# Reordering the second norm's transition: T4's products ahead of B22's, and the work of ScalarE, GpSimd and VectorE around them moved

## The chip, the cores and the metric

One core of one Trainium2 chip runs one launch of the kernel. The metric is the device time of the launch in microseconds. Before the change it is 1539.03 us, the median of three runs (1538.82 to 1541.5).

## What is computed

A bidirectional encoder block on one sequence of 1024 positions with 1024 channels, in float32. The change lies in its second half, the ConvFFN. Cut to that:

```python
h2 = rmsnorm(x, g_ffn) * (1 + scale2) + shift2
u = depthwise_conv_seq(h2 @ w_up, conv_w, conv_b)      # w_up: 1024 x 5632, 3 taps over positions
u_val, u_gate = jnp.split(u, 2, axis=-1)               # 2 x 2816 channels
x = x + gate2 * ((jax.nn.gelu(u_gate, approximate=True) * u_val) @ w_down)
return rmsnorm(x, g_final)
```

`scale2`, `shift2` and `gate2` come from the conditioning vector. `x` has by then the first half (two attentions, gates, `w_out`) added to it.

## The kernel before

**Precision.** A float32 product is made of three matmuls: each operand is split into a high part in fp32r (a copy on ScalarE) and a low part (operand minus high part, on VectorE or GpSimd), and TensorE (PE) adds high by high, high by low and low by high. `split` (lines 55 and 56) does this for weights.

**The up products.** `h2 @ w_up` runs as 22 jobs. A job makes 128 value channels and 128 gate channels of `u` for all 1024 positions, which are two halves of 512. So it is a 2 x 2 block product: weights a11, a12 (value) and a21, a22 (gate), the input halves over channels as blocks B11, B21 (first 512 positions) and two more blocks for the other positions. The kernel uses Strassen's scheme in Winograd's form, with seven block products in place of eight. The weight side needs S1 = a21 + a22, S2 = S1 - a11, S3 = a11 - a21 and S4 = a12 - S2, made on GpSimd (`FirstParts.sums`, `third`, `fourth`, lines 909, 910, 913 and 916, and `a_operands`, lines 884 to 886 and 891, for the later jobs). The input side needs T1, T2, T3, T4 and B22. The table `STEPS` pairs them: step 0 is a11 by B11, 1 is S2 by T2, 2 is S1 by T1, 3 is S3 by T3, 4 is a12 by B21, 5 is S4 by B22, 6 is a22 by T4. Each step is 12 matmuls of 128 x 512 in four chunks `k` (lines 950 to 952).

**PSUM.** `products` gives a job four banks, a to d, by the string `"abcdacd"`: step 5 adds onto the bank c that step 2 filled, and step 6 onto the bank d of step 3. Before step 5 may write, VectorE must have read step 2's value (line 963: `psum + v`, put into a spare bank); before step 6, it must have read step 3's (line 960, which makes `v`). After step 5 comes line 968, after step 6 line 971.

**The transition.** Jobs 0 and 1 start while the second half of the norm's input is still coming out of `w_out`. Their products run in lockstep, two generators `gens[0]` and `gens[1]`, in the order of steps 0, 4, 1, 3, 2, 5, 6, because T1 to T4 and B22 depend on the last sum of squares. `out_tile` finishes `m2[k]`, the second half of positions, unscaled; `scaled(k)` multiplies it by the norm's factor `bc`; `copied(k)` puts `m1[k]` (first half, scaled) into PSUM as `t2[k]`; `t2_sum` and `t2_low` make T2's high and low part, `t1_sum` and `t1_low` T1's, `t3_high` and `t3_low` T3's, `b22` (through `shifted`, lines 1078 and 1079) B22's, and `t4_sum` and `t4` (through `operand`, lines 864 and 865) T4's. The whole stretch is in `manual_schedule`: PE, ScalarE (ACT), VectorE (DVE) and GpSimd (POOL) each run their instructions in the order in which the code issues them, so the list of calls after `p0, p1 = first2` is the order on four engines at once. The queue of SyncE (SP), which issues the DMAs, is ordered by the scheduler. `advance(g)` and `next(g)` issue the next half or the rest of a step of a generator.

**The end of jobs 0 and 1.** `conv_in` (line 1163, ScalarE) and six taps (line 1169, VectorE) make the convolution of one half of the channels from four banks, line 1198 the Gelu of the gate half, line 1203 the gate times the value, line 1204 its store. `convs` holds four such pieces to be issued later; `held` keeps job 0's end until job 1's is done. Job 2 (`p2`) loads its two weight tiles into the slots that job 1's `raw[1]` tiles (`wraw`) leave. Jobs 3 to 21 and the product with `w_down` come after `late_others.close()`: there the scheduler orders ScalarE, VectorE and GpSimd by its own costs.

Of the kernel before, what the change touches and what calls it, by code (L numbers as in the profile page):

```python
# [10 lines left out]
FR = mybir.dt.float32r  # L11
AF = mybir.ActivationFunctionType
OP = mybir.AluOpType
# [3 lines left out]
S = 1024  # L17
# [11 lines left out]
def hybrid_encoder(tc, xT, c, w_ada, small, w_in, w_v, p1_bias, p23_bias, na_bias, ln2_mult, ident, w_br, w_out,  # L29
# [1117 lines left out]
    m2.append(half_tile())  # L1147
# [11 lines left out]
    with tc.tile_pool(name="up", bufs=2, reuse_waits="tile") as work:  # L1159
        held, convs = [], []  # L1160
# [16 lines left out]
        def up_products(t, st, seq=range(7)):  # L1177
            u, ys = [{}, {}], {i: big([128, S]) for i in range(2) if t == FF - 1}

            def done(i, hf, src):  # L1180
                u[i][hf] = src
                if len(u[i]) == 1 and t < 2:
                    return
                if t < 2:
                    convs.append(lambda: finish(i, hf))
                    return
                with tc.high_priority(offset=-300 if t == FF - 1 else 0):
                    finish(i, hf)

            def finish(i, hf):  # L1190
                if i not in ys:
                    ys[i] = big([128, S])
                for n in range(2) if t < 2 else (hf,):
                    conv_in(ys[i], up_order[t] + FF * i, n, u[i][n])
                if len(u[i]) == 2:
                    conv_taps(ys[i], up_order[t] + FF * i, u[i])
                if len(u[0]) + len(u[1]) == 4:
                    act.activation(ys[1], ys[1], AF.Gelu_apprx_tanh)  # L1198
                    if t == 0:
                        held.append((t, ys))  # L1200
                        return
                    for n, y in (*held, (t, ys)):
                        dve.tensor_tensor(y[0], y[0], y[1], OP.mult)  # L1203
                        sp.dma_start(a_scr[up_order[n]], y[0])
                    held.clear()
            spot, orders = None, {}
            if t < 2:
                spot, orders = (lambda: ps.tile([128, 512], FT, name="stage", tag=("pcol", "pbc")[t])), {2: (0, 2, 3, 1)}
            return products(st, 4, lambda n, k: late[n][k] if n in late else (ops[n][0][:, k], ops[n][1][:, k]), done,
                            seq, spot, orders)  # L1210

        gens = [up_products(t, sts[t], (0, 4, 1, 3, 2, 5, 6)) for t in range(2)]
# [26 lines left out]

        def t1_sum(k):  # L1240
            act.activation(m1[k], t2[k], AF.Copy)
            scaled(4 + k)
# [35 lines left out]
        copied(2)  # L1278
        scaled(0)
# [4 lines left out]
        p1.split_s(work)  # L1284
# [6 lines left out]
        pool.tensor_tensor(m2[3], m2[7], m2[3], OP.subtract)  # L1291
        p0.split_s3([work.tile([128, 2, 4, 128], FR, name=t, bufs=3) for t in ("wsh", "wsl")])
# [6 lines left out]
        p1.third()  # L1299
# [4 lines left out]
        t3_low(1)  # L1304
        t2_sum(3)
        t3_high(2)
        t2_low(3)
        t3_high(3)
        t3_low(2)
        advance(gens[0])  # L1310
        p1.split_s3(w_pair(4))
# [4 lines left out]
        p0.fourth()  # L1316
        p1.fourth()
        t1_sum(2)
        p0.split_s4()
        p1.split_s4()  # L1320
        t4_sum(0)
        t1_low(2)
        t1_sum(3)
        t4_sum(2)
        t1_low(3)
        t4_sum(3)
        t1_sum(1)
        t4_sum(1)
        advance(gens[0])
        t1_low(1)  # L1330
        advance(gens[1])
        next(gens[0])
# [11 lines left out]
        for k in range(4):  # L1344
            t4(k)
        next(gens[0])
        next(gens[1])
# [3 lines left out]
        convs.pop(0)()  # L1351
        p2.split_s(work)
        p2.split_s3([work.tile([128, 2, 4, 128], FR, name=t, bufs=3) for t in ("wsh", "wsl")])
        advance(gens[0])
        convs.pop(0)()
        p2.fourth()
        p2.split_s4()
        advance(gens[1])
        convs.pop(0)()
        convs.pop(0)()  # L1360
# [231 lines left out]
```

## Time and profile before

| | |
|---|---|
| median of three runs | 1539.03 us (1538.82 to 1541.5) |
| the profiled execution | 1538.77 us, its span 1537.0 us |
| PE busy | 1486.2 us, 97% of the span |
| VectorE, ScalarE, GpSimd busy | 992.0, 809.4 and 785.3 us (65%, 53%, 51%) |
| granted TensorE clock, mean | 0.986 |
| the transition | from 863 us of the span on; job 2's first product starts at 913.91 us |

The page gives busy time by engine over the whole span. PE is the engine that is nearly always busy, so time is lost where PE waits, and the views by window show where that is. A timeline row has the start, the duration, the line, the operation and its tiles, and in brackets how long the engine was idle before it and what ended that. Line numbers in rows are those of the kernel before.

### The profile page before, as it was taken

The page shows a single profiled execution, that of the slowest core. Times are in us where ns is not written, and L with a number is a line of the kernel's source. Part 1 is how long each engine was busy: PE and PEld are TensorE (multiplying, and loading weights), DVE is VectorE, ACT ScalarE, POOL GpSimd, SP SyncE. Part 2 cuts the span into 40 slices and gives each one's busy share as a digit, 9 for nine tenths or more (in the row PEclk, how much of TensorE's full clock was granted, in tenths as well). Part 3 has the DMA queues.
Part 4 walks back from the last instruction along what each step waited for, and adds up shares of the span by engine and source line. Part 5 has one row for each costly group of instructions (what it writes and reads, how often), then busy time and mean ns, then how long its engine had stood idle before and what let it go on. Part 6 is the DMA issues. An engine that isn't in the chain of part 4 may idle for free.

```text
span 1537.0 us, 21099 instructions
## 1 busy us (share of the span) xinstructions
PE 1486.2 (97%) x7512; PEld 1254.6 (82%) x7512; DVE 992.0 (65%) x1855; ACT 809.4 (53%) x1470; POOL 785.3 (51%) x506
## 2 busy tenths in 40 slices
PE   6999999999999999999999999999999999999998
PEld 5778888888888998888778777888888887878777
DVE  6673457676766655535534677777767778787765
ACT  5553656565765666644345545444444447476542
POOL 3524434333224444311156788877666675878721
PEclk7899999999999999999999999999999999999999
DMA  9857234423445565555544212322222224614323
GB/s 341 329 217 266 71 102 130 113 74 107 120 112 140 146 163 138 179 167 199 190 130 142 85 54 98 110 83 82 96 90 83 82 76 171 216 52 143 98 55 110
DMA packets 110305, 205.98 MB, mean 134 GB/s; under 512 B 40276, under 2 KB 55508, under 8 KB 110164
## 3 DMA queue, kind: packets, MB, share of 16 engines
q1 hardware_dynamic: 109928, 204.38, 41.0%
q8 instruction: 59, 0.97, 0.3%
q14 instruction: 46, 0.38, 0.1%
q10 hardware_dynamic: 272, 0.26, 0.0%
HBM read 159.51 MB, written 42.47 MB: 131 GB/s over the span
## 4 chain that ended last, share of the span: by engine, by line
PE 76%; DVE 7%; POOL 5%; DMA 4%; ACT 4%; issue 3%; SPq 1%; DVEq 0%; POOLq 0%; ACTq 0%
PE pj L79 11%; PE pj L78 11%; PE pj L77 11%; PE pj L952 9%; PE pj L951 9%; PE pj L950 9%; PE pj L467 2%; PE O L768 2%; POOL wlo L56 2%; DMA wraw<-w_down 2%; PE T L756 1%; PE b L247 1%; PE b L248 1%; PE S L735 1%; PE b L249 1%
## 5 line engine op out<-in xcount | busy, mean ns | idle before, releaser
L56 POOL TENSOR_TENSOR wlo<-wraw,whi 128x1024 fp32r<-128x1024 f32 (+1 forms) x80 | 188.2, 2353 | 225.3 <-ACT whi L55 224.1
L78 PE MATMUL pj<-h,whi 128*128 128x512 f32 x448 | 178.0, 397 | 0.0
L79 PE MATMUL pj<-h,wlo 128*128 128x512 f32 x448 | 178.0, 397 | 0.0
L77 PE MATMUL pj<-h,whi 128*128 128x512 f32 x448 | 177.9, 397 | 0.0
L1169 DVE SCALAR_TENSOR_TENSOR big<-pj,sm,big 128x512 f32<-128x512 f32 (+2 forms) x258 | 132.1, 566 | 31.3 <-ACT big L1163 31.1
L56 POOL TENSOR_TENSOR wsl<-big,wsh 128x1024 fp32r<-128x1024 f32 (+1 forms) x44 | 107.5, 2443 | 49.8 <-ACT wsh L55 49.8
L1163 ACT ACTIVATE big<-pj,sm 128x512 f32<-128x512 f32 x86 | 64.7, 776 | 118.9 <-DVE pj L968 51.8
L55 ACT ACTIVATE whi<-wraw 128x1024 fp32r<-128x1024 f32 (+1 forms) x80 | 81.8, 1022 | 85.0 <-PE pj L78 35.6
L79 PEld LDWEIGHTS pj<-h,wlo 128*128 128x128 f32 x448 | 84.4, 188 | 14.4
L78 PEld LDWEIGHTS pj<-h,whi 128*128 128x128 f32 x448 | 84.4, 188 | 14.1
L77 PEld LDWEIGHTS pj<-h,whi 128*128 128x128 f32 x448 | 84.3, 188 | 13.7
L538 POOL TENSOR_TENSOR vv<-vv 96x256 fp32r<-96x256 f32 (+2 forms) x32 | 41.2, 1297 | 98.8 <-ACT vv L537 97.6
L594 ACT ACTIVATE P<-P,st 128x256 f32<-128x256 f32 x128 | 64.3, 503 | 51.1 <-DVE st L593 50.8
L593 DVE CUSTOM_DVE_ANT_0 P<-S,bias 128x256 f32<-128x256 f32 x128 | 52.4, 421 | 42.7 <-PE S L640 23.8
L746 POOL TENSOR_SCALAR P<-P,stb 128x288 f32<-128x288 f32 (+1 forms) x32 | 39.9, 1247 | 66.4 <-DVE stb L743 59.2
L55 ACT ACTIVATE wsh<-big 128x1024 fp32r<-128x1024 f32 (+1 forms) x44 | 44.2, 1005 | 44.6 <-POOL big L885 26.2
L474 POOL TENSOR_SCALAR qb<-qs 128x256 fp32r<-128x256 f32 x32 | 26.4, 850 | 71.6 <-PE S L640 58.7
L1203 DVE TENSOR_TENSOR big<-big 128x1024 f32<-128x1024 f32 x22 | 45.7, 2076 | 22.0 <-ACT big L1198 22.0
L891 DVE TENSOR_TENSOR wraw<-wraw,big 128x384 f32<-128x384 f32 (+1 forms) x20 | 33.0, 1650 | 41.2 <-POOL big L885 39.6
L599 DVE TENSOR_TENSOR tl<-T,th 128x512 fp32r<-128x512 f32 x64 | 43.7, 688 | 23.4 <-ACT th L598 22.9
L950 PE MATMUL pj<-T2hi,wsh 128*128 128x512 f32 x124 | 48.8, 394 | 4.5 <-ACT T2hi L1234 3.2
L56 POOL TENSOR_TENSOR wsl<-wraw,wsh 128x768 fp32r<-128x768 f32 (+1 forms) x22 | 50.5, 2298 | 4.4 <-ACT wsh L55 4.4
(389 smaller groups left out, 4794.1 us busy)
## 6 DMA issues: line engine op xcount, KB each, us to landing
t<-w_ada SPq DMA_DIRECT2D x40, 512.0 KB, 6.7
wraw<-w_in SPq DMA_DIRECT2D x32, 512.0 KB, 5.6
big<-w_up SPq DMA_DIRECT2D x22, 512.0 KB, 5.0
wraw<-w_up SPq DMA_DIRECT2D x22, 512.0 KB, 3.6
as<-big SPq DMA_DIRECT2D x22, 512.0 KB, 2.6
big<-as SPq DMA_DIRECT2D x22, 512.0 KB, 6.9
wraw<-w_down SPq DMA_DIRECT2D x24, 384.0 KB, 4.1
gs<-gs SPq DMA_DIRECT2D x32, 256.0 KB, 2.0
```

The lines of the kernel that those rows point to most:

```text
L55: act.activation(hi, raw, AF.Copy)
L56: lo_eng.tensor_tensor(lo, raw, f(hi), OP.subtract)
L77: pe.matmul(psum, whi[:, k0 + k], mhi, start=k == 0, stop=False)
L78: pe.matmul(psum, whi[:, k0 + k], mlo, start=False, stop=False)
L79: pe.matmul(psum, wlo[:, k0 + k], mhi, start=False, stop=k == n - 1)
L593: dve.tensor_tensor_reduce(pp, d, bias, -1.0, BIG, OP.add, OP.min, mi)
L594: act.activation(pp, pp, AF.Exp, bias=mi, scale=-1.0, accum_out=li)
L950: pe.matmul(psum, whi[:, k], bhi, start=j < 4 and i == 0, stop=False, skip_group_check=True)
L951: pe.matmul(psum, whi[:, k], blo, start=False, stop=False, skip_group_check=True)
L952: pe.matmul(psum, wlo[:, k], bhi, start=False, stop=i == n - 1, skip_group_check=True)
L1163: act.activation(y[:, halves[hf]], src, AF.Identity, bias=conv[:, 3, t:t + 1], scale=conv[:, 1, t:t + 1])
L1169: dve.scalar_tensor_tensor(y[:, dst], src, wt, y[:, dst], OP.mult, OP.add)
```

## The change

The seven steps of jobs 0 and 1 now run in the order 0, 4, 1, 3, 2, 6, 5, so T4's products come before B22's. T4's parts are issued before B22's on ScalarE and GpSimd, and `fourth` and `split_s4` (S4 of both jobs) after T4's. `third` and `split_s` of job 1 and `split_s3` of both jobs are issued earlier, the copies that keep `m1[k]` (`t2_kept`, part of `t1_sum` before) in one group, the scaling of `m2[4..7]` earlier than the T1 sums that read it. `m2[7]` lies in a tile of `wide` in place of `half_tile`. The convolutions' parts are now four dictionaries: `cins` (copies), `taps`, `gelus`, `ends2` (gate and store), issued in a new interleaving with job 2's weights, the gate half of each job first. No instruction is added or left out: each engine issues as many as before.

```diff
--- before.py
+++ after.py
@@ -1144,7 +1144,7 @@
     late_others.enter_context(tc.manual_schedule(engines={act.engine, dve.engine, pool.engine}))
     first2[1].sums()
     first2[1].split11(pool)
-    m2.append(half_tile())
+    m2.append(wide())
     sq = out_tile(1, KT - 1, sqa, m2[KT - 1])
     mpool.release()
     oppool2 = tc.alloc_tile_pool(name="ops2", bufs=1, side="right", reuse_waits="tile")
@@ -1157,7 +1157,11 @@
     late = {n: [] for n in ("B22", "T4")}
 
     with tc.tile_pool(name="up", bufs=2, reuse_waits="tile") as work:
-        held, convs = [], []
+        cins, taps, gelus, ends2 = {}, {}, {}, {}
+
+        def gated(t, ys):
+            dve.tensor_tensor(ys[0], ys[0], ys[1], OP.mult)
+            sp.dma_start(a_scr[up_order[t]], ys[0])
 
         def conv_in(y, t, hf, src):
             act.activation(y[:, halves[hf]], src, AF.Identity, bias=conv[:, 3, t:t + 1], scale=conv[:, 1, t:t + 1])
@@ -1182,7 +1186,11 @@
                 if len(u[i]) == 1 and t < 2:
                     return
                 if t < 2:
-                    convs.append(lambda: finish(i, hf))
+                    ys[i] = big([128, S])
+                    cins[t, i] = lambda: [conv_in(ys[i], up_order[t] + FF * i, n, u[i][n]) for n in range(2)]
+                    taps[t, i] = lambda: conv_taps(ys[i], up_order[t] + FF * i, u[i])
+                    gelus[t] = lambda: act.activation(ys[1], ys[1], AF.Gelu_apprx_tanh)
+                    ends2[t] = lambda: gated(t, ys)
                     return
                 with tc.high_priority(offset=-300 if t == FF - 1 else 0):
                     finish(i, hf)
@@ -1190,26 +1198,19 @@
             def finish(i, hf):
                 if i not in ys:
                     ys[i] = big([128, S])
-                for n in range(2) if t < 2 else (hf,):
-                    conv_in(ys[i], up_order[t] + FF * i, n, u[i][n])
+                conv_in(ys[i], up_order[t] + FF * i, hf, u[i][hf])
                 if len(u[i]) == 2:
                     conv_taps(ys[i], up_order[t] + FF * i, u[i])
                 if len(u[0]) + len(u[1]) == 4:
                     act.activation(ys[1], ys[1], AF.Gelu_apprx_tanh)
-                    if t == 0:
-                        held.append((t, ys))
-                        return
-                    for n, y in (*held, (t, ys)):
-                        dve.tensor_tensor(y[0], y[0], y[1], OP.mult)
-                        sp.dma_start(a_scr[up_order[n]], y[0])
-                    held.clear()
+                    gated(t, ys)
             spot, orders = None, {}
             if t < 2:
                 spot, orders = (lambda: ps.tile([128, 512], FT, name="stage", tag=("pcol", "pbc")[t])), {2: (0, 2, 3, 1)}
             return products(st, 4, lambda n, k: late[n][k] if n in late else (ops[n][0][:, k], ops[n][1][:, k]), done,
                             seq, spot, orders)
 
-        gens = [up_products(t, sts[t], (0, 4, 1, 3, 2, 5, 6)) for t in range(2)]
+        gens = [up_products(t, sts[t], (0, 4, 1, 3, 2, 6, 5)) for t in range(2)]
 
         def advance(g):
             for j in g:
@@ -1237,9 +1238,10 @@
             dve.scalar_tensor_tensor(ops["T2"][1][:, k], t2[k], shift2[:, 4 + k:5 + k], f(ops["T2"][0][:, k]), OP.add,
                                      OP.subtract)
 
+        def t2_kept(k):
+            act.activation(m1[k], t2[k], AF.Copy)
+
         def t1_sum(k):
-            act.activation(m1[k], t2[k], AF.Copy)
-            scaled(4 + k)
             dve.tensor_tensor(t2[k], m2[4 + k], t2[k], OP.subtract)
             act.activation(ops["T1"][0][:, k], t2[k], AF.Copy)
 
@@ -1276,59 +1278,68 @@
         advance(gens[0])
         bc = bcast(r, ps, "pbc")
         copied(2)
+        p1.third()
+        p1.split_s(work)
         scaled(0)
         t2_sum(0)
         scaled(1)
         t2_sum(1)
         advance(gens[1])
-        p1.split_s(work)
+        pool.tensor_tensor(m2[3], m2[7], m2[3], OP.subtract)
+        p0.split_s3([work.tile([128, 2, 4, 128], FR, name=t, bufs=3) for t in ("wsh", "wsl")])
         t2_low(0)
         scaled(2)
         t2_sum(2)
         t2_low(1)
         advance(gens[0])
         advance(gens[1])
-        pool.tensor_tensor(m2[3], m2[7], m2[3], OP.subtract)
-        p0.split_s3([work.tile([128, 2, 4, 128], FR, name=t, bufs=3) for t in ("wsh", "wsl")])
+        t2_kept(0)
+        scaled(4)
         t1_sum(0)
         t2_low(2)
         t1_low(0)
         copied(3)
         next(gens[0])
         next(gens[1])
-        p1.third()
         scaled(3)
         t3_high(0)
         t3_high(1)
         t3_low(0)
         t3_low(1)
+        p1.split_s3(w_pair(4))
         t2_sum(3)
         t3_high(2)
+        t3_high(3)
+        scaled(6)
         t2_low(3)
-        t3_high(3)
+        for k in (2, 3, 1):
+            t2_kept(k)
+        for k in (0, 2, 3, 1):
+            t4_sum(k)
         t3_low(2)
         advance(gens[0])
-        p1.split_s3(w_pair(4))
         t3_low(3)
         advance(gens[1])
         next(gens[0])
         next(gens[1])
-        p0.fourth()
-        p1.fourth()
         t1_sum(2)
-        p0.split_s4()
-        p1.split_s4()
-        t4_sum(0)
+        scaled(7)
         t1_low(2)
         t1_sum(3)
-        t4_sum(2)
+        scaled(5)
         t1_low(3)
-        t4_sum(3)
         t1_sum(1)
-        t4_sum(1)
+        t4(0)
+        t4(1)
         advance(gens[0])
         t1_low(1)
         advance(gens[1])
+        t4(2)
+        t4(3)
+        p0.fourth()
+        p1.fourth()
+        p0.split_s4()
+        p1.split_s4()
         next(gens[0])
         next(gens[1])
         b22(0)
@@ -1341,23 +1352,27 @@
         p2 = FirstParts(raw.pop(2), sts[2])
         p2.sums()
         p2.third()
-        for k in range(4):
-            t4(k)
-        next(gens[0])
-        next(gens[1])
         p2.split11(pool)
         advance(gens[0])
         advance(gens[1])
-        convs.pop(0)()
+        cins[0, 1]()
+        taps[0, 1]()
+        cins[1, 1]()
         p2.split_s(work)
+        advance(gens[0])
+        taps[1, 1]()
         p2.split_s3([work.tile([128, 2, 4, 128], FR, name=t, bufs=3) for t in ("wsh", "wsl")])
-        advance(gens[0])
-        convs.pop(0)()
+        advance(gens[1])
+        cins[0, 0]()
+        gelus[0]()
+        taps[0, 0]()
+        cins[1, 0]()
+        gelus[1]()
+        taps[1, 0]()
         p2.fourth()
         p2.split_s4()
-        advance(gens[1])
-        convs.pop(0)()
-        convs.pop(0)()
+        ends2[0]()
+        ends2[1]()
         late_others.close()
         for t in range(FF):
             nxt = iter(())
```

Three places in the built order. GpSimd, from job 1's S3 on (`wsl`, `wlo` and the split `big` tiles are low parts of weights, line 1261 or 1263 the four T4 sums, line 865 T4's low parts, line 909 job 2's first sum). Before:

```order
L913 TENSOR_TENSOR wraw_8352<-wraw_8350,wraw_8352 128x512
L56 TENSOR_TENSOR wlo_8567<-wraw_8352,whi_8566 128x1024
L916 TENSOR_TENSOR big_8229<-big_8229,big_8354 128x512
L916 TENSOR_TENSOR wraw_8350<-wraw_8350,big_8366 128x512
L56 TENSOR_TENSOR big_8598<-big_8229,big_8598 128x512
L56 TENSOR_TENSOR big_8601<-wraw_8350,big_8601 128x512
L1261 TENSOR_TENSOR big_7742<-big_7742,big_7740 128x512
L1261 TENSOR_TENSOR big_7743<-big_7743,big_7741 128x512 x2
L1261 TENSOR_TENSOR big_7742<-big_7742,big_7740 128x512
L909 TENSOR_TENSOR big_8685<-wraw_8683 128x512
L910 TENSOR_TENSOR big_8685<-big_8685,wraw_8681 128x512
L913 TENSOR_TENSOR wraw_8683<-wraw_8681,wraw_8683 128x512
```

Now:

```order
L913 TENSOR_TENSOR wraw_8352<-wraw_8350,wraw_8352 128x512
L56 TENSOR_TENSOR wsl_8468<-big_8366,wsh_8467 128x1024
L1288 TENSOR_TENSOR x2_8191<-wc_8373,x2_8191 128x512
L56 TENSOR_TENSOR wsl_8494<-big_8231,wsh_8493 128x1024
L56 TENSOR_TENSOR wlo_8554<-wraw_8352,whi_8553 128x1024
L1263 TENSOR_TENSOR big_7742<-big_7742,big_7740 128x512
L1263 TENSOR_TENSOR big_7743<-big_7743,big_7741 128x512 x2
L1263 TENSOR_TENSOR big_7742<-big_7742,big_7740 128x512
L865 TENSOR_TENSOR x2_8611<-big_7742,x2_8610 128x512
L865 TENSOR_TENSOR x2_8615<-big_7742,x2_8614 128x512
L865 TENSOR_TENSOR x2_8636<-big_7743,x2_8635 128x512
L865 TENSOR_TENSOR x2_8640<-big_7743,x2_8639 128x512
```

L913 has moved ahead of the low part of job 1's S2, the T4 sums ahead of the two L916 (S4), and T4's four low parts, which followed job 2's weight sums, ahead of S4 as well; S4's two differences and their low parts, and then job 2's weights, come after these rows.

ScalarE, at the high parts of T1, T4 (line 864) and B22 (line 1078); the `big` rows of line 55 are S4's high parts. Before:

```order
L55 ACTIVATE big_8598<-big_8229 128x512
L55 ACTIVATE big_8601<-wraw_8350 128x512
L1241 ACTIVATE big_7741<-pj_8531 128x512
L1244 ACTIVATE T1hi_8410<-pj_8531 128x512
L1241 ACTIVATE big_7740<-stage_8449 128x512
L1244 ACTIVATE T1hi_8410<-stage_8449 128x512
L1078 ACTIVATE x2_8649<-x2_8233,ada_66 128x512
L1078 ACTIVATE x2_8653<-x2_8272,ada_66 128x512
L1078 ACTIVATE x2_8665<-x2_8311,ada_66 128x512
L1078 ACTIVATE x2_8677<-x2_8373,ada_66 128x512
L864 ACTIVATE x2_8689<-big_7742 128x512
L864 ACTIVATE x2_8693<-big_7742 128x512
```

Now:

```order
L1246 ACTIVATE T1hi_8410<-stage_8449 128x512
L864 ACTIVATE x2_8610<-big_7742 128x512
L864 ACTIVATE x2_8614<-big_7742 128x512
L864 ACTIVATE x2_8635<-big_7743 128x512
L864 ACTIVATE x2_8639<-big_7743 128x512
L55 ACTIVATE big_8645<-big_8229 128x512
L55 ACTIVATE big_8648<-wraw_8350 128x512
L1078 ACTIVATE x2_8665<-x2_8233,ada_66 128x512
L1078 ACTIVATE x2_8669<-x2_8272,ada_66 128x512
L1078 ACTIVATE x2_8681<-x2_8311,ada_66 128x512
L1078 ACTIVATE x2_8693<-wc_8373,ada_66 128x512
L55 ACTIVATE whi_8705<-wraw_8697 128x1024
```

S4's high parts and B22's four rows stood ahead of T4's and now follow them; the copies of line 1241 that stood between T1's rows are gone from here.

SyncE's queue, the weight loads of jobs 2 (the first two rows), 3 (`big`) and 4 (`wraw_8820`, `wraw_8822`). Before:

```order
L1108 DMA wraw_8681<-w_up 128x1024
L1108 DMA wraw_8683<-w_up 128x1024
L1108 DMA wraw_8820<-w_up 128x1024
L1108 DMA wraw_8822<-w_up 128x1024
L1108 DMA big_8816<-w_up 128x1024
L1108 DMA big_8818<-w_up 128x1024
```

Now:

```order
L1108 DMA wraw_8697<-w_up 128x1024
L1108 DMA wraw_8699<-w_up 128x1024
L1108 DMA wraw_8820<-w_up 128x1024
L1108 DMA big_8816<-w_up 128x1024
L1108 DMA big_8818<-w_up 128x1024
L1108 DMA wraw_8822<-w_up 128x1024
```

Job 3's two loads have moved ahead of job 4's second.

## The prediction

> **What bounds the kernel now.** I read the page first, then PE's windows and waits, then one engine at a time. The page names the engine that matters, by busy time and by the chain that ended last:
>
> ```profile
> PE 1486.2 (97%) x7512; PEld 1254.6 (82%) x7512; DVE 992.0 (65%) x1855; ACT 809.4 (53%) x1470; POOL 785.3 (51%) x506
> PE 76%; DVE 7%; POOL 5%; DMA 4%; ACT 4%; issue 3%; SPq 1%; DVEq 0%; POOLq 0%; ACTq 0%
> ```
>
> So only time in which PE stands still, or runs at a lower clock, can go. By window (the transition in two parts, then steady jobs):
>
> ```profile
> core 0: us, PE busy (x) PEld busy (x) DVE busy (x) ACT busy (x) POOL busy (x), PEclk, DMA share, GB/s
> 863.20:902.00 38.80, 32.90 (x144) 26.17 (x143) 29.08 (x39) 23.91 (x39) 30.08 (x19) 0.96 0.10 34
> 902.00:946.00 44.00, 41.96 (x175) 33.52 (x175) 31.97 (x53) 23.38 (x29) 33.22 (x18) 0.96 0.28 96
> 960.00:1060.00 100.00, 100.00 (x443) 82.81 (x442) 71.57 (x105) 44.88 (x54) 73.15 (x40) 1.00 0.27 90
> ```
>
> Steady jobs leave PE no gap: 443 matmuls in 100 us, 0.226 us each. The transition leaves 38.80 - 32.90 = 5.9 and 44.00 - 41.96 = 2.0 us. PE's waits there, 863 to 946 (total, times, longest), and their places in its timeline:
>
> ```profile
> PE pj L950 <- ACT T2hi L1234: 3.2, 1, 3.2
> PE pj L950 <- DVE stage L963: 2.4, 1, 2.4
> PE pj L950 <- ACT wc L956: 1.1, 1, 1.1
> PE pj L952 <- POOL wsl L56: 0.7, 1, 0.7
> 883.14 0.50 PE L950 MATMUL pj<-T2hi,wsh 128*128 128x512 f32 x1 [3.15 <-ACT T2hi L1234]
> 885.18 0.63 PE L950 MATMUL pj<-T2hi,wsh 128*128 128x512 f32 x1
> 888.60 0.39 PE L952 MATMUL pj<-T3hi,wsl 128*128 128x512 f32 x1
> 901.28 0.47 PE L950 MATMUL pj<-x,big 128*128 128x512 f32 x1 [2.35 <-DVE stage L963]
> 902.29 0.63 PE L951 MATMUL pj<-x,big 128*128 128x512 f32 x1
> 905.68 0.40 PE L950 MATMUL pj<-x,big 128*128 128x512 f32 x1
> 914.36 0.39 PE L952 MATMUL pj<-B11hi,wlo 128*128 128x512 f32 x1
> ```
>
> Two waits matter: T2's last chunk, and S4 by B22 waiting for VectorE's line 963. Behind each a stretch of 3.4 us runs at half rate (0.63 us a matmul, 885.18 to 888.60 and 902.29 to 905.68), which costs 1.7 us each. 914.36 is job 2's third matmul, the first that needs its `wlo`; I measure the change there, because everything before it is jobs 0 and 1.
>
> **The first wait.** The chain behind it, on VectorE, GpSimd and ScalarE:
>
> ```profile
> 875.45 0.70 DVE L1243 TENSOR_TENSOR pj<-x,pj 128x512 f32<-128x512 f32 x1 [0.98 <-ACT big L1241]
> 878.01 3.74 DVE L1253 SCALAR_TENSOR_TENSOR T3lo<-x,cols,T3hi 128x512 fp32r<-128x512 f32 x2
> 881.68 0.69 DVE L1233 TENSOR_TENSOR pj<-pj,x 128x512 f32<-128x512 f32 x1
> 883.79 0.74 DVE L1253 SCALAR_TENSOR_TENSOR T3lo<-x,cols,T3hi 128x512 fp32r<-128x512 f32 x1
> 877.12 2.42 POOL L56 TENSOR_TENSOR wsl<-big,wsh 128x1024 fp32r<-128x1024 f32 x1
> 879.48 1.73 POOL L913 TENSOR_TENSOR wraw<-wraw 128x512 f32<-128x512 f32 x1
> 873.86 1.07 ACT L55 ACTIVATE wsh<-big 128x1024 fp32r<-128x1024 f32 x1
> ```
>
> Two T3 low parts, 0.74 us alone, took 3.74: they span the two GpSimd operations (to 879.54, and 879.48 to 881.21) and end after them; the T2 sum follows at 881.68. The new order puts L913 and `p1.split_s` earlier, and ScalarE's copy of 873.86 ahead of the T2 and T1 copies. VectorE's 0.98 of waiting at 875.45 falls away, so the T3 low parts start at 877.06; GpSimd is then idle, until ScalarE has written the high part of job 1's S3, some 878.4. The two take 2 x 0.66, the T2 sum starts at 878.4, T2's high part is there at 879.8 by the same distance as before (881.68 to 883.14), its low part 0.7 later. PE is ready for the high part at 883.14 - 3.15 = 880.0 and one matmul later, at 880.2, for the low part: a wait of 0.3 in place of 3.15, none if VectorE is a little earlier, all of it back if GpSimd again overlaps. I take 0.3, since the overlap is gone from the order.
>
> **PE up to S4.** From 880.5 it has 8 matmuls of T2, then 24 each of T3, T1 and T4: 80 x 0.226 = 18.1. It wants B22's step at 898.6.
>
> **GpSimd up to S4.** This engine has the longest list. Its rows of before, and the ScalarE and VectorE rows that stand between:
>
> ```profile
> 888.23 1.28 POOL L916 TENSOR_TENSOR big<-big 128x512 f32<-128x512 f32 x1
> 893.25 5.04 POOL L1261 TENSOR_TENSOR big<-big 128x512 f32<-128x512 f32 x4
> 903.31 5.47 POOL L865 TENSOR_TENSOR x<-big,x 128x512 fp32r<-128x512 f32 x4
> 908.74 2.42 POOL L56 TENSOR_TENSOR wlo<-wraw,whi 128x1024 fp32r<-128x1024 f32 x1
> 898.39 1.66 ACT L864 ACTIVATE x<-big 128x512 fp32r<-128x512 f32 x3
> 897.28 3.24 DVE L1079 SCALAR_TENSOR_TENSOR x<-x,ada,x 128x512 fp32r<-128x512 f32 x2
> 900.45 0.69 DVE L963 TENSOR_TENSOR stage<-pj,wc 128x512 f32<-128x512 f32 x1
> 909.28 3.09 DVE L1169 SCALAR_TENSOR_TENSOR big<-pj,sm,big 128x512 f32<-128x512 f32 x6
> ```
>
> Job 1's S3 low part runs 878.4 to 880.8, the four T4 sums (5.04, with 0.45 twice for overlap, as L913 took 1.73 where L916 takes 1.28) to 886.7. T4's first high part cannot start before ScalarE has copied T1's k=1, whose sum is VectorE's eleventh operation after 880.5 (0.6 to 0.7 apart, about 7.5): 888.0, plus 0.6 and 0.55 (1.66 / 3): 889.1. Now GpSimd runs without a pause: four line-865 low parts 5.0 to 894.1, two L916 2.5 to 896.6. Then S4's high part and B22's first high parts on ScalarE (0.63 + 0.64) to 897.9, two B22 low parts on VectorE, L963 behind them. GpSimd makes S4's low parts at that moment, so the pair costs between 1.4 (alone) and 3.24 (as at 897.28); I take 2.4. L963 ends at 897.9 + 2.4 + 0.7 = 901.0 and PE waits 901.0 - 898.6 = 2.4, just as long as before: L963 still stands behind two B22 low parts. B22's 24 matmuls take 5.4, or 7.1 with a slow stretch: job 2's third matmul could start at 906.9 to 908.6.
>
> **Job 2's weights.** More rows, for the next parts: the gate product, a wait of the taps for ScalarE, the S4 low part of job 2, job 3's load and what it held up, and the loads of `w_up` (KB, median us to landing):
>
> ```profile
> L1203 DVE TENSOR_TENSOR big<-big 128x1024 f32<-128x1024 f32 x22 | 45.7, 2076 | 22.0 <-ACT big L1198 22.0
> 928.20 0.75 DVE L1169 SCALAR_TENSOR_TENSOR big<-pj,sm,big 128x512 f32<-128x512 f32 x1 [2.52 <-ACT big L1163]
> 918.02 1.29 POOL L56 TENSOR_TENSOR big<-wraw,big 128x512 fp32r<-128x512 f32 x1 [0.90 <-ACT big L55]
> 919.76 6.06 DMA big<-w_up
> 929.20 2.41 POOL L56 TENSOR_TENSOR wlo<-big,whi 128x1024 fp32r<-128x1024 f32 x1 [9.88 <-ACT whi L55]
> wraw<-w_up SPq DMA_DIRECT2D x22, 512.0 KB, 3.6
> ```
>
> S4's low parts end at 896.6 + 2.5 = 899.1 and free the second load slot; a load takes 3.6 (last row), 902.8; L909, L910 and L913 3.8, 906.6; `wlo` 2.42, 909.0. GpSimd ends later than PE, so job 2's third matmul starts at 909.0 in place of 914.36: 5.4 earlier. The bounds: at PE's 906.9 it is 7.5. With 0.45 of overlap in each of four operations it is 3.6, and with 6.06 for the load in place of 3.6 also, 1.1. I take 5.4, because the load moves 512 KB with the queue otherwise empty there (10% DMA share in the first window).
>
> The rule in the Trainium skill's "SBUF — State Buffer" (section "Who interferes with whom") is that VectorE and GpSimd share one port pair under an exclusive lock. The rows at 878.01 and 879.48 agree (3.74 for 1.4, 1.73 for 1.28). By it B22's third and fourth low parts could hold GpSimd up once more, 2 x 0.74, and job 2's gain would be 3.9, between the forecast and the second rival.
>
> **VectorE in job 2.** Now all 24 taps are run straight after B22, and two gate products (L1203) stand between job 2's line 958 and 963. From 901.0: two B22 low parts and a L963 1.9, two L971 1.2, 0.9 for ScalarE's copies, 24 taps 12.0 (3.0 between six at 909.28), two L968, a L958 and a L960 2.4, two products 2.4, L963 0.7: 922.5. PE's step 5 of job 2, 58 matmuls after the third, stands at 909.0 + 13.1 = 922.1. That costs 0.4, or nothing, or 2.2 if the products run at their mean. So two chains, GpSimd's and VectorE's, allow about the same gain.
>
> The L1203 row's 2076 is the mean ns; I counted 1.2, two inputs of 1024 columns against 0.69 for 512, as no GpSimd work that overlaps is sure to be due then.
>
> **Job 3 and later.** SP issued job 3's loads at 919.76, behind a load of job 4 that waited for job 2's S4 low part (918.02); GpSimd then stood idle for 9.88. Now they go ahead of it, as soon as job 2's `wlo` and two `wsl` are done, 909.0 + 2 x 2.4 = 913.8: 5.9 earlier, with PE 5.0 earlier. The two waits at the next hand-over (1.1 + 0.7) stay: 0, bounds -1.5 to +2. `m2[7]`'s other tile and the order that the scheduler gives jobs 3 to 21 cost nothing while PE is covered as in 960:1060; after them 0, bounds -2 to +2.
>
> **Sum.** -5.4 + 0.4 = -5.0. The profiled execution took 1538.77, so 1533.8; the median (1539.03) stands 0.26 above it: 1534.0.
>
> **Rivals.**
> 1. *Faster still.* The lists of GpSimd and VectorE both run some 2 us shorter, and PE's floor of 906.9 (gain 7.5) or, with no wait at S4, 904.5 (9.9) holds: 1531.5 or 1529.1. For it: GpSimd's overlaps were guessed. Against: both have to give.
>    Does the 2.4 us wait slow PE's clock here? In the rows above, gaps of 3.15 and 2.35 were both followed by a slow stretch; with one, this rival's gain is 5.8. "TensorE: Matmul & The Clock Gate" in the Trainium skill (section "HAM oscillation") has as its rule that only gaps over some 3.4 us matter; by it the gain would be 7.5 in full. The trace disagrees.
> 2. *Same.* T2's wait comes back, or the load takes 6.06: gain 1 to 3, 1536 to 1538. For it: GpSimd has no slack in the list above, each lock adds 0.45.
> 3. *Slower.* VectorE is the bound. If each of the four groups of taps waits for ScalarE as at 928.20 (2.52), and the products run at 2.08, VectorE's L963 of job 2 comes 10.1 + 1.7 later, 934.3; PE waits 12.2 there, of which 5.4 were gained: 1539.0 + 6.8 = 1545.8. It decides from 927.5 on, where before's PE stood at this step. Against it: all copies are issued ahead of their taps, and ScalarE was 23.38 busy of 44.
>
> **Chances.** Forecast 0.70 (1532 to 1536), rival 1 0.10, rival 2 0.15, rival 3 0.05. The range runs from half of rival 1 to most of rival 2, 1530.0 to 1537.5. What the measurement tells from no change is about 0.2%, 3.1 us: forecast and rival 1 are faster by that (0.80), rival 2 is the same (0.15), rival 3 slower (0.05).
>
> **What would show it.** Right: PE's wait at T2's k=3 under 1 us and no slow stretch at 885; a wait of 1.5 to 3 us on L963 at the start of the last B22 step; the four line-865 rows on GpSimd without a gap before S4's; job 2's third matmul 4.5 to 6 us earlier than 914.36; SP's `big` loads near 914. Wrong: a T3 low part of over 1.5 us, a w_up load of over 5 us near 899, or a wait on L963 or L960 in job 2's steps 5 and 6.

## The result

The first comparison has six runs of each kernel: 1530.26 us median (1527.08 to 1531.87) after, 1539.25 (1538.82 to 1541.5) before, ratio 0.9936, interval 0.9922 to 0.9951. That is 9.0 to 9.9 us faster, where 5.0 was forecast; by the ratio the time is 1529.2 to 1529.4, some 0.7 below the lower end of the range. The same kernel was run twice more (e5_again, e11_third below): 0.9968 and 0.9974. All 28 runs of it have a mean of 1532.4 (standard deviation 2.9), 78 runs of the kernel before 1538.2 (2.2): 5.8 us apart, with 1.2 either way (twice the root of 2.9²/28 + 2.2²/78). By comparison the means lie 9.8, 5.2 and 4.2 us apart. The last two were made on two different chips, and that of the first is not on record; what a chip adds was not tested.

The profiled execution of the changed kernel took 1531.87, span 1530.1, that is 6.9 us less. Busy time on its page, by engine:

```profile
PE 1484.6 (97%) x7512; PEld 1254.6 (82%) x7512; DVE 964.2 (63%) x1855; ACT 807.9 (53%) x1470; POOL 777.9 (51%) x506
```

The two windows of the transition, columns as in the prediction (span, PE busy, and so on to the clock):

```profile
863.20:902.00 38.80, 36.08 (x159) 28.94 (x158) 26.79 (x41) 23.72 (x39) 30.30 (x20) 0.98 0.10 34
902.00:946.00 44.00, 42.65 (x179) 33.37 (x178) 36.13 (x54) 25.06 (x31) 40.28 (x23) 0.98 0.31 109
```

PE's waits from 863 to 946 us (total, times, longest):

```profile
PE pj L950 <- ACT x L1078: 2.4, 1, 2.4
PE pj L950 <- DVE wc L960: 0.7, 1, 0.7
PE pj L951 <- DVE T2lo L1238: 0.3, 1, 0.3
PE pj L950 <- DVE big L1173: 0.3, 1, 0.3
PE pj L952 <- POOL wsl L56: 0.2, 1, 0.2
```

PE's idle time fell from 5.9 and 2.0 to 2.7 and 1.35 us, and T2's 3.15 is gone. The 2.4 is the wait at S4 by B22: the copy of line 1078 that it names is the fourth (to 899.98), while the product begins with the first chunk; line 963, done at 899.83, frees its bank. The 0.7 for line 960 comes at 943.08, in job 3. The rows of its timeline behind that, several engines in order of time (line numbers of the changed kernel, each some lines off the old ones):

```profile
875.44 1.41 DVE L1255 SCALAR_TENSOR_TENSOR T3lo<-x,cols,T3hi 128x512 fp32r<-128x512 f32 x2
876.97 2.39 POOL L56 TENSOR_TENSOR wlo<-wraw,whi 128x1024 fp32r<-128x1024 f32 x1 [2.05 <-ACT whi L55]
879.33 5.96 POOL L1263 TENSOR_TENSOR big<-big 128x512 f32<-128x512 f32 x4
887.98 5.04 POOL L865 TENSOR_TENSOR x<-big,x 128x512 fp32r<-128x512 f32 x4 [2.70 <-ACT x L864]
896.83 2.40 DVE L1079 SCALAR_TENSOR_TENSOR x<-x,ada,x 128x512 fp32r<-128x512 f32 x2 [8.12 <-ACT x L1078]
899.15 0.68 DVE L963 TENSOR_TENSOR stage<-pj,wc 128x512 f32<-128x512 f32 x1
899.99 0.59 PE L950 MATMUL pj<-x,big 128*128 128x512 f32 x1 [2.44 <-ACT x L1078]
901.54 1.34 POOL L909 TENSOR_TENSOR big<-wraw 128x512 f32<-128x512 f32 x1 [3.52 <-DMA wraw<-w_up]
905.47 2.41 POOL L56 TENSOR_TENSOR wlo<-wraw,whi 128x1024 fp32r<-128x1024 f32 x1
907.93 0.50 PE L952 MATMUL pj<-B11hi,wlo 128*128 128x512 f32 x1
```

The two T3 low parts take 1.41 in place of 3.74, since GpSimd is idle until 876.97. Read the GpSimd rows downwards: S3's low part, T4's sums, T4's low parts, then S4's differences (to 895.52) and low parts (to 898.02), a wait of 3.52 for job 2's load, job 2's sums and its `wlo` to 907.88, and PE's first use of that at 907.93, in job 2's third matmul.

To compare executions I cut each at four places. *Entry* is the start of the transposes that spread the norm's factor for the first half of the positions (827.75 us before); the change touches little ahead of it. *Lead* is how far ahead PE then is in the steady jobs: matmuls counted from there on, against the same stretch of before, times 0.2267 us. *Later* is what is added up to the last norm's first narrow matmul (1500.75 before), *end* the rest. All in us against the profile of before, negative is faster; a count can be off by one matmul.

| kernel | entry | lead | later | end |
|---|---|---|---|---|
| changed, first profile | -1.7 | -5.0 | -3.2 | +3.0 |
| changed, e5_again | +0.5 | -5.0 | -2.9 | 0.0 |
| changed, e11_third | -2.9 | -5.0 | -1.2 | +1.4 |
| e1 early moves only | -0.2 | -3.8 | -0.4 | 0.0 |
| e6 new ending only | +2.1 | -2.5 | -1.2 | +0.2 |
| e9 step order only | -3.4 | +3.8 | -3.1 | 0.0 |
| e7 early moves and ending | -1.8 | -4.3 | +1.0 | -0.1 |
| e3 early moves and order | +1.7 | +0.3 | -1.5 | +0.1 |
| e2 order and ending | +1.1 | -0.8 | -0.3 | -0.1 |
| e8 T4's low parts on VectorE | -3.6 | -9.2 | -2.4 | -0.2 |
| e10 the same, two more moves | -0.2 | -9.7 | -2.9 | -0.1 |

The lead is the same 5.0 in three profiles. What differs between runs lies outside it. (e4 has no row: its narrow matmuls at the end are fewer; its lead is 4.7.)

### The profile page after: what moved, and what is told of

Same layout as the page of the kernel before. It is cut to its first block, busy times and chain, and to the rows that moved or that the text cites. A ratio compares the mean times of both kernels' runs of the same rounds, so it can differ in the third digit from the quotient of the medians.

```text
span 1530.1 us, 21118 instructions
## 1 busy us (share of the span) xinstructions
PE 1484.6 (97%) x7512; PEld 1254.6 (82%) x7512; DVE 964.2 (63%) x1855; ACT 807.9 (53%) x1470; POOL 777.9 (51%) x506
## 4 chain that ended last, share of the span: by engine, by line
PE 74%; POOL 8%; DVE 6%; issue 4%; DMA 4%; ACT 3%; SPq 0%; DVEq 0%; POOLq 0%; ACTq 0%
PE pj L79 11%; PE pj L77 11%; PE pj L78 11%; PE pj L952 8%; PE pj L950 8%; PE pj L951 8%; POOL wsl L56 2%; PE pj L467 2%; PE O L768 2%; POOL wlo L56 2%; DMA wraw<-w_down 2%; PE T L756 1%; PE S L735 1%; PE b L247 1%; PE b L249 1%
## 5 line engine op out<-in xcount | busy, mean ns | idle before, releaser
L968 DVE TENSOR_TENSOR pj<-pj,wc 128x512 f32<-128x512 f32 x34 | 23.6, 694 | 52.0 <-PE pj L952 51.9
L79 PE MATMUL pj<-mhi,wlo 128*128 128x512 f32 x128 | 50.2, 392 | 2.0 <-POOL wlo L56 2.0
L78 PE MATMUL pj<-mlo,whi 128*128 128x512 f32 x128 | 50.0, 391 | 0.0
```

The costliest lines, as they stand in the source:

```text
L78: pe.matmul(psum, whi[:, k0 + k], mlo, start=False, stop=False)
L79: pe.matmul(psum, wlo[:, k0 + k], mhi, start=False, stop=k == n - 1)
```

## The experiments

**The three parts of the change, one at a time.** `first_only` is the kernel before with the early moves:

```diff
         copied(2)
+        p1.third()
+        p1.split_s(work)
...
         advance(gens[1])
-        p1.split_s(work)
+        pool.tensor_tensor(m2[3], m2[7], m2[3], OP.subtract)
+        p0.split_s3([...])
         t2_low(0)
```

(with `third` and the last two lines taken from their old places, and `m2[7]` in a tile of `wide`).

> The kernel before with the early moves alone: L913 and the split of job 1's S2, and the split of job 0's S3, earlier, and the last tile in its new place; B22 still ahead of T4, the old ending. Lead is counted from PE's place at 863 us to its place in the steady jobs, 960 to 1290 us; the changed kernel has 5.0 there. Theory of the prediction (two lists, GpSimd's to job 2's first low part and VectorE's with the taps, bound the start and the middle of job 2, and T2's wait only starts them earlier): the wait at T2's k=3 falls from 3.15 to under 0.5, the wait on L963 stays 2 to 2.6, the lead is 3 to 3.5, since everything after T2 starts that much earlier in the old order too. Rival 1 (the step order 6, 5 makes the gain): the lead is under 1.5, the T2 time comes back as a longer wait on L963. Rival 2 (T2's wait with its slow stretch is the whole gain): 4.5 to 5.

Measured: ratio 0.9986 (0.9974 to 0.9999), 1535.4 median of 12 runs. Lead 3.8. Its largest waits from 863 to 955 us:

```profile
PE pj L950 <- ACT x L864: 2.6, 1, 2.6
PE pj L950 <- DVE wc L958: 1.6, 1, 1.6
```

T2's wait is gone, 1.6 of it is back as a wait for VectorE's line 958, and the wait at S4 by B22 is as before (the row names line 864; line 963 is what must be read there). No stretch runs at half clock, where the kernel before had two of 1.7 us each: 3.4 of the lead's 3.8 is that. The lead lies above the theory's 3 to 3.5 and below the second rival's 4.5 to 5: T2's wait with its slow stretch is not the whole gain, and more than the theory had comes with it.

`second_only` is the changed kernel with these moves undone (the same lines, the other way; `m2[7]` stays in its tile of `wide`).

> The changed kernel with the early moves undone: L913, job 1's S2 split, the T4 difference of m2 and job 0's S3 split back at their old places; the steps 0, 4, 1, 3, 2, 6, 5, T4 ahead of S4, and the new ending stay. Theory: T2's wait is back at 3.15 with its slow stretch at 885, GpSimd's list starts some 3.5 us later, and the lead from 863 to 960 us is 1.5 to 2; a wait of 1 to 3 us at job 2's start on its weights. Rival 1 (the step order makes the gain): 3.5 or more. Rival 2 (T2 is the whole gain): 0 within 0.5.

Measured: ratio 0.9985 (0.9972 to 0.9997). Lead 0.8, between the theory and the second rival. T2's wait returns with its half-clock stretch, and GpSimd's list is late: S4's second difference ends at 902.22, 3.9 us later than in the changed kernel with the entries (2.8 apart) taken off. That is met once more at job 2's start, in the second row (what ended that wait is taken up behind the experiments):

```profile
PE pj L950 <- ACT T2hi L1235: 3.1, 1, 3.1
PE pj L950 <- ACT wsh L55: 1.5, 1, 1.5
```

`old_end` is the changed kernel with copies, taps and Gelus interleaved as before:

```diff
         taps[0, 1]()
-        cins[1, 1]()
         p2.split_s(work)
-        advance(gens[0])
-        taps[1, 1]()
         p2.split_s3([...])
-        advance(gens[1])
+        advance(gens[0])
+        cins[1, 1]()
+        taps[1, 1]()
+        p2.fourth()
+        p2.split_s4()
+        advance(gens[1])
         cins[0, 0]()
...
```

> The changed kernel with the copies, taps and Gelus of jobs 0 and 1 in the old interleaving (job 0, then job 1's after the next step, the Gelus last); all ahead of job 2's weights as in the changed kernel. The prediction counted 0.4 us for VectorE's list and said that it allows about the same gain as GpSimd's list. Theory, sharpened: the banks that job 2's steps 1 and 2 need are freed by taps, so ScalarE's copies standing behind job 2's splits hold them up; a wait of 3 to 5 us in job 2 on a tap (L1172/L1173) and a lead of 0 to 1.5 in place of 5.0. Rival (GpSimd's list alone bounds; the ending is free): lead 4.5 to 5, no wait over 1 us in job 2.

Measured: ratio 0.9989 (0.9976 to 1.0002), its lead 0.3 behind before. PE's largest group of waits from 863 to 946 us:

```profile
PE pj L950 <- DVE big L1173: 6.7, 3, 4.4
```

PE, VectorE and ScalarE in its timeline at the longest of the three:

```profile
922.05 0.50 PE L950 MATMUL pj<-T1hi,wsh 128*128 128x512 f32 x1 [4.36 <-DVE big L1173]
919.29 3.10 DVE L1173 SCALAR_TENSOR_TENSOR big<-pj,sm,big 128x512 f32<-128x512 f32 x6 [0.79 <-POOL big L56]
917.22 0.63 ACT L55 ACTIVATE big<-wraw 128x512 fp32r<-128x512 f32 x1 [2.73 <-POOL wraw L916]
917.75 1.43 ACT L1167 ACTIVATE big<-pj,sm 128x512 f32<-128x512 f32 x2
```

ScalarE's copies (line 1167) stand behind the high part of job 2's S4, that waits 2.73 for GpSimd; the taps wait for the copies, and job 2's T1 step for the bank that the taps read. So the new ending is what makes the new step order pay.

`end_only` is the kernel before with the new ending, value half first; `first_and_end` has both; `order_only` is `second_only` with the ending of `old_end`.

> The kernel before (steps 5, 6; the first wait as it was) with the new ending alone: copies, taps, Gelus and gates of jobs 0 and 1 in the new interleaving, here value half first, since step 5 completes it first. Theory (the ending only serves the new step order: in the old order no tap frees a bank late): lead 0.5 to 1.7, the waits at job 3's start (1.06, 0.33, 0.66) partly gone, T2's 3.15 and the L963 wait unchanged. Rival (the ending is worth its own gain in any order): lead 3 or more. And for the stretch from 1290 to 1480 us: if the new ending's code is what changes the order there, it gains 1.5 to 3 as in the kernels with the new code; else it is as in the kernel with the early moves alone (0.4).

Measured: 1537.34 in one run, lead 2.5, between the two. T2's 3.1 and a wait of 2.6 for line 963 stand as before, but only T2's is followed by half clock here, which is 1.7 of the 2.5. Compared matmul by matmul with the profile of before, it gains 2.2 from 1290 to 1480 us, having lost 1.0 between 1100 and 1150. That is in the range expected if the ending's code changes the order there; but e7, with the same ending, loses 0.3 in the same stretch.

> Early moves and new ending together, with B22 ahead of T4 as in the kernel before. Theory (the early moves are worth 3.8 in the old order, the new step order adds the rest and needs the new ending): lead 4.0 to 5.3, so at most 1 us is left for the step order. Rival (the new step order is worth more than 1.5 by itself): lead under 3.5.

Measured: 1533.56 in one run, lead 4.3, inside the theory. The step order is worth 0.7 us in the transition once the two others are there.

> The kernel with the new step order alone: steps 0, 4, 1, 3, 2, 6, 5 with T4's parts ahead of S4's and B22's on ScalarE and GpSimd, without the early moves (T2's wait stays) and with the copies, taps and Gelus in the old interleaving. It completes the table of the three parts. Theory (the step order alone takes the banks' taps away from job 2 and leaves T2's wait): lead -2.5 to -4.5, that is, slower than the kernel before by as much at 960 us: waits of some 3.1 at T2, 1.5 to 2 at S4 by B22, 1.5 at job 2's weights and over 4 on a tap in job 2. Rival (the parts add up): -0.8 from the kernel without the early moves and the old ending's 5 together, i.e. the same sign but under 2 us.

Measured: 1536.07 in one run, its lead 3.8 behind before (its total is shorter by its entry and by *later*): at 960 us the step order alone is that much slower than the kernel before, and one wait in its timeline has 4.4:

```profile
921.03 0.79 PE L950 MATMUL pj<-T1hi,wsh 128*128 128x512 f32 x1 [4.38 <-DVE big L1173]
```

The parts do not add up: in the table's signs, -3.8 (early), -2.5 (ending) and +3.8 (order) make -2.5, the whole -5.0.

**GpSimd's list or VectorE's?** T4's four low parts go to VectorE:

```diff
-            operand(m1[4 + k], *late["T4"][k], pool)
+            operand(m1[4 + k], *late["T4"][k], dve)
...
+        t1_low(1)
         t4(0)
         t4(1)
         advance(gens[0])
-        t1_low(1)
```

> The changed kernel with T4's four low parts made on VectorE in place of GpSimd (line 865's engine), and T1's last low part issued ahead of them. In the changed kernel VectorE stands idle 8.12 us there (before 896.83) while GpSimd runs T4's low parts (5.04), then S4's parts, and then waits 3.52 for job 2's second load, whose slot S4's low part frees. Theory (GpSimd's list bounds job 2's start and S4 by B22): S4 is made some 4 to 5 us earlier, the wait of 2.44 at S4 by B22 is under 0.5, job 2 starts with no wait over 0.5, lead 8.5 to 9.5 in place of 5.0, time 3.5 to 4.5 under the changed kernel's. Rival 1 (VectorE's list of taps bounds, as the prediction had it, 0.4 us behind GpSimd's): lead 5.0 to 6.5, a wait on L960, L963 or a tap in job 2. Rival 2 (VectorE's T4 parts hold up T1's or T4's matmuls): a wait of 1 to 3 us at T4's step.

Measured: 1528.07 median, ratio to before 0.994 (0.9927 to 0.9952), where the changed kernel had 0.9968 on the same chip. Lead 9.2. PE's waits from 863 to 946:

```profile
PE pj L950 <- ACT wsh L55: 0.8, 1, 0.8
PE pj L950 <- DVE big L1173: 0.6, 1, 0.6
PE pj L950 <- DVE wc L960: 0.3, 1, 0.3
```

GpSimd's first S4 difference and job 2's first sum in its timeline:

```profile
883.38 1.30 POOL L916 TENSOR_TENSOR big<-big 128x512 f32<-128x512 f32 x1
894.71 1.28 POOL L909 TENSOR_TENSOR big<-wraw 128x512 f32<-128x512 f32 x1 [3.52 <-DMA wraw<-w_up]
```

S4 is made from 883.38 where it was 892.98 (7.7 us earlier with this execution's earlier entry taken off), job 2's load is there 6.8 us earlier (4.9 so), the 2.44 at S4 is gone, and no stretch of the transition runs at half clock. The theory's lead came out; two waits of over 0.5 are left where it had none, and the median lies 5.5 under the changed kernel's (4.3 by the ratios) where it had 3.5 to 4.5. Both rivals' times are out, but VectorE, which took T4's low parts over (4.5 us), is not idle in this: job 2's first matmul, at 901.91, starts 0.15 behind a tap of VectorE (901.76), when GpSimd's `wlo` is done (901.31).

`t4_dve_b` also issues GpSimd's S4 differences ahead of T4's last operands and line 963 ahead of B22's low parts.

> The kernel with T4's low parts on VectorE (lead 9.24) with two more moves: GpSimd's S4 differences issued ahead of T4's last two operands, and line 963 of both jobs ahead of B22's low parts on VectorE. Theory (what is left there, 0.81 on ScalarE's copy of job 2's weights, 0.65 on a tap, 0.34 on line 960, 2.1 in all with T2's 0.28, goes in part): lead 9.5 to 10.5, time 1525 to 1529, not to be told from the kernel with T4 on VectorE alone. Rival (line 963 ahead of the B22 low parts makes these late): a wait of over 1 us at S4 by B22, lead under 9.

Measured: 1527.14 median, ratio 0.9926 (0.9908 to 0.9943), lead 9.7, waits of 0.66, 0.44 and 0.28 left. This is the fastest version, though not to be told from e8 by time.

**Why runs differ.** `end_half` adds one more square tile on GpSimd (`elif m < 7` in place of `m < 6`), so that the narrow matmuls over it fall away.

> The changed kernel; in the last norm GpSimd adds one more tile of squares, so TensorE's sums over it (narrow matmuls, one column of ones each, 16 in a row in 1.84 us and 8 more 1.4 us later in the trace of the changed kernel) are 8 and 8. Theory (the half-clock stretch at 1495 to 1501 us, which the profiled execution shows and which costs it 2.6 us, comes from that run of narrow matmuls, in some executions only): the stretch is gone, the runs lie within 1.5 us of each other, at 1527 to 1529. Rival (it comes from something else, a phase or a state of the execution): the runs still spread over 4 to 5 us, from 1527 to 1532.

Measured: 1527.9 to 1534.19 in six runs, ratio 0.9953 (0.9935 to 0.9972). The rival: the spread stays, though its profile has no slow stretch at this place. In the first profile of the changed kernel 1495 to 1500 us reads

```profile
1495.00:1500.00 5.00, 5.00 (x25) 5.00 (x25) 1.19 (x4) 1.04 (x3) 0.72 (x1) 0.50 0.00 0
```

and in e5_again

```profile
1495.00:1500.00 5.00, 5.00 (x44) 5.00 (x44) 1.10 (x4) 1.46 (x4) 0.65 (x1) 1.00 0.01 3
```

The same program, PE busy throughout (5.00 of 5.00), half clock in one execution (the 3.0 of *end*) and full clock in the other (the column before the last two). Whether the narrow matmuls cause it stays open.

> The changed kernel as it is, beside more runs of the kernel before on the same chip: 29 runs of the kernel before have by now spread from 1533.9 to 1542.6, so its six runs say too little. Theory: lead of the transition 4.7 to 5.1 again (PE's place at 863 to the steady jobs); from 1290 to 1480 us the changed kernel gains 2 to 3 more, as it did in its first profile (3.2) and with one changed sum at the end (2.0); the median lies 6.5 to 8.5 us under before's. Rival (the 9 us were the place where few runs fell): 4.5 to 5.5 in all, the part behind 1290 us within 1 us of nothing.

Measured: 1533.61 median, ratio 0.9968 (0.9953 to 0.9982). Lead 5.0 and 2.9 more up to the last norm, as the theory has it; the median is the rival's, 4.5 us under before's.

> The changed kernel a third time: its first six runs gave a ratio of 0.9936, ten more gave 0.9968, and these two intervals hardly meet. Theory (one effect of some 7 us, 5.0 in the transition and 2 to 3 behind 1290 us, seen through executions that differ by 2 to 3 us among themselves): ratio 0.994 to 0.997, median 1530 to 1534; the profile again shows a lead of 5.0 and 2.5 to 3.5 more up to the last norm. Rival (two different states of the kernel, one 5 us faster than the other): runs in two groups with a gap of over 3 us between them.

Measured: 1533.26 median, ratio 0.9974 (0.9958 to 0.9989), the runs in one group from 1529.86 to 1537.95. Ratio just over the theory's, *later* only 1.2.

## Why the prediction was right or wrong

**The first wait: right.** 0.28 on T2's low part in place of 3.15 (0.3 forecast), by the way forecast.

**GpSimd's list: right up to job 2's weights.** With the entry's 1.7 added back, the first profile has T4's sums ending at 887.0 (forecast 886.7), S4's differences at 897.2 (896.6), line 963 at 901.5 (901.0), job 2's load at 903.2 (902.8), its `wlo` at 909.6 (909.0). The wait at S4 was 2.44 (2.4). Job 3's `big` loads were issued at 913.00, with the entry 914.7 (913.8).

Some of this agreement is luck. The 2.4 for two B22 low parts was a choice between 1.4 and 3.24, and they took 2.40. The lead was 5.0 (5.0), but job 2's third matmul came 4.75 earlier where the sum has 5.4, the 0.4 for VectorE was not paid, and two waits at the next hand-over that the sum left as they were (1.06 and 0.66 before) came down to one of 0.23, with 0.68 on line 960 behind it.

That PE does not set job 2's start is seen best where the clock differed. The window behind the wait at S4, first profile:

```profile
900.00:905.00 5.00, 5.00 (x15) 3.96 (x16) 4.01 (x7) 3.54 (x5) 3.38 (x3) 0.66 0.15 60
```

the same in e11_third:

```profile
900.00:905.00 5.00, 4.46 (x20) 3.37 (x18) 3.98 (x8) 3.82 (x6) 4.60 (x4) 1.00 0.00 0
```

and several engines in e11_third's timeline at job 2's start, first and third matmul:

```profile
905.97 0.47 PE L950 MATMUL pj<-B11hi,whi 128*128 128x512 f32 x1 [1.51 <-ACT wsh L55]
898.68 1.04 ACT L55 ACTIVATE whi<-wraw 128x1024 fp32r<-128x1024 f32 x1
904.79 1.06 ACT L55 ACTIVATE wsh<-wraw 128x1024 fp32r<-128x1024 f32 x1
905.35 0.47 DVE L1173 SCALAR_TENSOR_TENSOR big<-pj,sm,big 128x255 f32<-128x255 f32 x1
904.27 2.39 POOL L56 TENSOR_TENSOR wlo<-wraw,whi 128x1024 fp32r<-128x1024 f32 x1
906.72 0.50 PE L952 MATMUL pj<-B11hi,wlo 128*128 128x512 f32 x1
```

The first profile has B22's step at 0.66 of full clock behind the 2.44 us wait; e11_third has full clock behind a wait of 2.40, and PE then waits 1.51. Both leads are 5.0. The row puts the 1.51 down to the copy of `wsh`, but this matmul reads `whi`, done at 899.72. The sixth tap on VectorE, which reads a bank `pj`, ended at 905.82. In the first profile, e2, e3, e5_again, e8 and e11_third alike this matmul starts about 0.15 behind that tap, and in e3, where `wsh` was done 0.5 ahead of the matmul, the profile names the tap. So VectorE's taps let the first matmul go, and GpSimd's `wlo` (to 906.66) holds the third for some 0.2 us more: two chains that end almost together. Both start at S4's differences on GpSimd. VectorE stood idle for 8.12 before B22's low parts, for copies that follow S4's on ScalarE, and works its way from there to the taps.

**VectorE in job 2: wrong in its reader, and missed at job 2's start.** The sum has no tap at job 2's first matmul. It lets PE's step 5 wait for line 963. In job 2 the steps run 2, 3, 5, and what step 5 needs is line 960 (timeline of the first profile):

```profile
918.79 0.68 DVE L960 TENSOR_TENSOR wc<-pj,wc 128x512 f32<-128x512 f32 x1
922.13 0.68 DVE L963 TENSOR_TENSOR pj<-pj,wc 128x512 f32<-128x512 f32 x1
922.67 0.39 PE L950 MATMUL pj<-x,big 128*128 128x512 f32 x1
```

It ended at 919.47, 3.2 us ahead of step 5, which starts before line 963 has ended, so the 0.4 was nothing. The first rival's "both have to give" did not hold at that place: in e8 VectorE's list is 4.5 longer and the lead went to 9.2, since S4 and with it the taps come earlier. The third rival's place was right for another kernel: taps that wait for ScalarE cost 4.4 in e3 and e9; I had not seen that the new ending is there to avoid that.

**The step that failed: after 960 us, "0, bounds -2 to +2".** The changed kernel was 3.2, 2.9 and 1.2 faster there. PE's waits from 1280 to 1480 us, the two largest groups, before:

```profile
PE pj L951 <- DVE B21l L1003: 1.6, 2, 1.4
PE pj L950 <- ACT wsh L55: 1.3, 2, 0.8
```

and its SP queue there (the last store of that stretch, the next pair of `w_down` loads):

```profile
1296.06 0.32 SPq L1204 DMA_DIRECT2D as<-big  x1
1299.59 2.31 SPq L1065 DMA_DIRECT2D wraw<-w_down  x2
```

The two largest groups of the first profile after:

```profile
PE pj L952 <- POOL wlo L56: 1.2, 1, 1.2
PE pj L950 <- ACT whi L55: 0.9, 2, 0.4
```

and its SP queue:

```profile
1282.14 0.32 SPq L1164 DMA_DIRECT2D as<-big  x1
1288.64 2.57 SPq L1065 DMA_DIRECT2D wraw<-w_down  x2
```

The store comes 13.9 us earlier and the pair of loads behind it 11.0, while PE is 6.7 earlier (entry and lead). The waits for B21's low parts are gone. They stand in all four kernels with the old step order (1.4, 1.4, 1.3 and 1.7 for the longest) and in none with the new one. Compared matmul by matmul with the profile of before, the stretch from 1300 to 1320 us is shorter in every profile with the new step order (1.7 in seven, 0.7 in e2 and e11_third) and 0.8 to 1.5 longer in the three others with the old one (e6 and e7 have a half-clock stretch there). So up to 1.7 of *later* goes with the step order, in jobs that the scheduler orders; I had put it at 0. The rest does not: from 1320 to 1480 us the three old-order kernels gain 1.2 to 3.0 on the profile of before, those with the new order from 1.5 down to a loss of 0.3. In all, *later* is 0.3 in e2 and 1.5 in e3, both with the new order, and 1.2 in e6 with the old. Why the scheduler's order changed, and whether the earlier loads took the waits away, was not tried.

**And the range.** It had no term for how executions of one program differ. The three runs shown lay within 2.7 us of each other; 78 runs of the kernel before go from 1532.48 to 1542.55. Entry alone varies from -3.6 to +2.1 in the table, ahead of the change. Over 28 runs the gain is 5.8, inside the range. The mean of the first six lay 2.6 below that of the 28, and the six of before 1.4 above that of the 78, which turns 5.8 into 9.8: that is luck, or something that went with this comparison. Lead, *later* and *end* of the three profiles add up to 5.2, 7.9 and 4.8 us gained, near the 5.8.

**The clock rule.** By the Trainium skill's "TensorE: Matmul & The Clock Gate", section "HAM oscillation", the rule is to have no gaps on PE of over some 3.4 us. Taken as the length from which a gap slows PE, it does not fit these profiles: all six gaps of 3.12 to 4.38 us (before, e2, e3, e6, two in e9), four of them under 3.2, were followed by a half-clock stretch, and of the gaps of 2.35 to 2.62 some were (before, first profile, e5_again, e7) and some not (e1, e3, e4, e6, e11_third). One of only 1.52 was (e4, at 910 us), where one of 1.51 was not (e11_third).

## What to carry to other kernels

When steps are reordered, find for each engine the list that ends at the next stage's first need, and date every row of it; here five dates came out within 0.6 us. Check for each bank or tile which instruction really frees it in the new order, since a move that pays with its companion (-5.0) can cost 3.8 without it. Check for each wait whether what the profile names is something that the waiting instruction needs: here a copy of `wsh` stood for a tap. An order left to a scheduler has to be priced as a change too, and three runs do not show how far a program's executions spread.

## What the runs showed of the hardware

A wait of 2.4 us on PE was followed by 3.4 us at half clock in some executions of one program and not in others (first profile and e11_third, above), so a gap of this length cost 0 or 1.7 us more, in one execution or another. A half-clock stretch can also come with no gap on PE at all (1495 us, first profile). Where VectorE and GpSimd overlap, either may pay: two B22 low parts took 2.40 beside a GpSimd operation that kept its 1.29 (1.40 in e8, with GpSimd idle), while T4's four sums on GpSimd took 5.96 beside two T3 low parts of 1.04 and 1.19, and 5.04 before.
